# MoBA's scores and its PV products each in one run per layer, in a two-layer hybrid decoder trunk on one Trainium2 core

## The chip, the cores and the metric

The kernel runs on one core of a Trainium2 chip. The metric is the device time of one execution in microseconds (us); less is better. Five engines run side by side, each with its own program: PE (TensorE: matmuls, with weight loads shown apart as PEld), DVE (VectorE), ACT (ScalarE), POOL (GpSimd) and SP (SyncE, which here only issues DMAs). They meet through semaphores.

## The reference

Two layers, 256 tokens, width 1024, one sequence. In each layer one input projection feeds three groups of heads, and each group's output is gated and goes through one output projection:

```
h = rms_norm(x, norm_g[l])
q_a, k_a, v_a, q_h, f_h, i_h, q_m, z = split(h @ w_in[l])      # w_in: 1024 x 5120 -> seven parts of 512 and z of 1536
o_a = moba_attention(rope(norm(q_a)), rope(norm(k_a)), v_a)    # 8 heads x 64
o_h = rms_norm(hgrn2_chunkwise(q_h, f_h, i_h, lb))             # 4 heads x 128, a gated linear recurrence
o_m = memory_attention(norm(q_m), km, vm)                      # 4 heads x 128, keys and values from mem
x = x + (concat(o_a, o_h, o_m) * silu(z)) @ w_out[l]           # w_out: 1536 x 1024
```

MoBA lets a query see its own block of 256 keys, causally, and the best of the blocks that lie wholly in the past. With 256 tokens there is one block, so what is computed is causal attention: scores `q k^T`, a mask, softmax, and the product of the probabilities P with v (PV).

## The kernel before

**The stream of weights.** Every projection is done in three passes on weights and activations that are split into a high and a low part. A chunk of weights, 128 x 1024 f32 (512 KB), is loaded by SP (`wr`, L178), cast by ACT to its high part (`wh`, L214, or L218 with a gain), and the rest is taken by DVE (`wl`, L228 or L232). A layer has 60 such chunks: behind those of the memory's keys and values come, four each, HGRN's forget gate and q, MoBA's k, HGRN's i, MoBA's q, the gate of HGRN's branch (zh), the memory's q (qm), MoBA's v (va), the gates of MoBA's and of the memory's branch, and 12 of w_out. There are 4 buffers of raw chunks; the look-ahead is 5 chunks for loads, 3 for the high and 2 for the low part.

**Who sets the order.** `group_a` and `group_b` issue the projection matmuls (L276, 128x512 or 128x256, 128 rows by 128 columns of the array); `w_out_phase` issues those of the output projection (L1261). After each part they call `slot()`, which lets every waiting generator (`spawn`, `yield`, `reach(l, c)`: "from chunk c of layer l on") do its next piece. A scheduler then fixes each engine's program from this order and its own estimate of times; `mm_row` (L280) keeps a matmul at its place in the written order, `in_turn` adds edges that only order instructions of one engine, `issue_after` puts one instruction behind another. PSUM has 8 banks of 128x512: 4 `acc` for projections, 4 `sd` for all else.

**MoBA.** `g_moba` starts when q and k are normed and turned. Heads come in two units of 4; tokens t = 0 and t = 1 are the two halves of the sequence. The scores are f32 matmuls on 64 of the array's rows, two heads beside each other: 8 of 128x128 for t = 0 of all heads, then 4 of 128x256 for t = 1 of unit 0 (`second(0)`), all in four `sd` tiles. `g_moba_unit` of unit 1 issues its own 4 (`second(1)`) when two `sd` tiles are free again. DVE adds the mask and takes the maximum in one instruction (`masked`, L1033), then the bias `nba`; ACT takes the exponentials (L1068), DVE scales them (L1076) and transposes P in blocks of 32 (`blk`, L95). `across` sends `blk` through DRAM on POOL's queue: one store (L106), 768 KB, and four loads (L111) into `PT`. The PV products use 64 of the array's columns, again two heads beside each other: for each head one of 128x256 and one of 128x128, into one `sd` tile a unit. Unit 0's come from chunk 48 on, where the last projection has been issued, unit 1's from chunk 50 on, so in the middle of w_out. `y_store` gates the product and splits it for w_out (`ys`, `yh`, `yl`, L782 to L784).

**HGRN's output** `zh` takes the same way through DRAM (`y_turned`): its store and loads stand on POOL's queue between those of the first P (`turned0`) and those of the second (`turned1`), whose store waits for zh's loads to be issued (`behind=f"zh{l}moved"`). Transposed, zh is cast by ACT (L129) just ahead of w_out, whose first four chunks are HGRN's (`KT_ORDER` 4 to 7, then MoBA's 0 to 3, then the memory's 8 to 11). HGRN's matmuls with `ih` on one side and `hST` or `hX` on the other are f32 on the full array.

**The memory's attention** (`g_qm`, `g_mem_unit`) norms qm, scores it against the memory's keys, takes maxima on DVE (`mxm`, L1179), exponentials on ACT (L1186), and has its PV in the later part of w_out.

The functions that the change touches, and what calls them:

Of the kernel before, what the change touches and what calls it, by code (L numbers as in the profile page):

```python
# [28 lines left out]
EPS = 1e-6  # L29
# [16 lines left out]
def hymba_kernel(ctx: ExitStack, tc: tile.TileContext, x, mem, mem_t, positions, w_in, w_out, w_mem_kv,  # L46
# [41 lines left out]
    def across(dst, src, n, stage=None, free=None, name=None, q=None, behind=None):  # L88
        q = q or nc.sync
        if stage is None:  # L90
# [4 lines left out]
        nc.vector.transpose(blk.rearrange("p c (n i) -> p c n i", n=n),  # L95
                            src.rearrange("p (n c i) -> p c n i", n=n, c=4))
# [8 lines left out]
        with tc.issue_after(T[behind].ins) if behind is not None else nullcontext():  # L105
            q.dma_start(there.rearrange("q j c r -> (q j) c r"), blk)  # L106
        if stage is None:
            rel("blk")
        yield 4
        for c in (0, 2, 1, 3):  # L110
            ins = q.dma_start(dst[c * 32:c * 32 + 32], there[:, :, c].rearrange("q j r -> j q r"))  # L111
            if c == 2:
                yield
# [4 lines left out]
    def turned(a, stage=None, q=None, name=None):  # L118
        yield from across(a.rearrange("p (q r) -> p q r", q=4), a, 8, stage, q=q, name=name)
# [7 lines left out]
    def unstripped_high(oh, a):  # L127
        for t in range(2):
            T["ACT"] = nc.scalar.copy(strip_of(oh, t), strips(a)[:, :, t])  # L129
            tc.keep_in_program_order(T["ACT"])  # L130
# [76 lines left out]
    def h_to(n):  # L207
        while st["h"] < min(n, len(chunks)):
# [3 lines left out]
            if g is None:  # L212
                with behind("ACT"):
                    nc.scalar.copy(whs[i], raws[i])  # L214
            else:
                for sl in parts(i):
                    with behind("ACT"):
                        nc.scalar.activation(whs[i][:, sl], raws[i][:, sl], AF.Copy, scale=gT[:, g:g + 1])  # L218
# [119 lines left out]
    def group_a(thl, each):  # L338

        pair = None  # L340
        for h in range(4):
# [12 lines left out]
            spawn(g_sum(h, pair[:, (h % 2) * 256:(h % 2) * 256 + 256], acc, each(h - 1, pair) if h % 2 else None))  # L354
            slot(True)

    def g_sum(h, o, acc, then):
        lo = sb.tile([128, 256], F32, name="al", tag="al", bufs=2)
        nc.scalar.copy(lo, acc[:, 256:])
        N["sum", h] = T["sum"] = nc.vector.tensor_tensor(o, acc[:, :256], lo, op=OP.add)  # L360
# [262 lines left out]
    def sumsq(dst, acc, n):  # L623
        sq = sb.tile([128, 512], F32, name="sq", tag="sq", bufs=2)
        nc.scalar.activation(sq, acc, AF.Square)
        nc.vector.tensor_reduce(dst, heads(sq, n), AX.X, OP.add)

    def rsq(name, ss, n, width):
        ms = small(name + "m", n)
        nc.vector.tensor_scalar(ms, ss, 1.0 / width, EPS, op0=OP.mult, op1=OP.add)  # L630
# [116 lines left out]
    def g_va(l, acc):  # L747
        T["va"] = sb.tile([128, 2, 512], F32, name="va", tag="hq1", bufs=1)
        for t in range(2):
            nc.scalar.copy(T["va"][:, t], acc[t])  # L750
# [11 lines left out]
    def g_zt(l, br, h0, acc):  # L762
# [3 lines left out]
        with tc.issue_after(T["exp"].ins):  # L766
            nc.scalar.activation(sg, acc, AF.Sigmoid)
# [10 lines left out]
    def y_store(l, br, u, po):  # L778
        yh, yl = (a.rearrange("p k s -> p (k s)")[:, u * 512:(u + 1) * 512] for a in y_tiles(br))
        ys = sb.tile([128, 512], F32, name="ys", tag="sq", bufs=2)  # L780
        with tc.issue_after(T["sum"].ins):
            nc.vector.tensor_tensor(ys, po, zT[br][:, u * 512:(u + 1) * 512], op=OP.mult)  # L782
        nc.scalar.copy(yh, ys)
        nc.vector.tensor_tensor(yl, ys, yh.bitcast(F32), op=OP.subtract)  # L784
# [4 lines left out]
    def y_turned(l):  # L789
# [3 lines left out]
        yield from turned(flat, "hq0", nc.gpsimd, f"zh{l}")  # L793
# [9 lines left out]
    def g_hgrn(l):  # L803
# [145 lines left out]
        for t in range(2):  # L949
# [8 lines left out]
            sumsq(ss[:, t * 4:t * 4 + 4], o, 4)  # L958
# [3 lines left out]
        for t in range(2):  # L962
            for h in range(4):
                z = zh[:, t, h * 128:(h + 1) * 128]
                nc.vector.scalar_tensor_tensor(z, in0=po[t][:, h * 128:(h + 1) * 128],
# [65 lines left out]
    def masked(P, i, t, s, mx):  # L1031
        c, nk = t * 4 + i, 128 * (t + 1)
        nc.vector.tensor_tensor_reduce(out=P[:, i, kc[t]], in0=s, in1=cm[:, 256 - nk:], scale=1.0, scalar=-3e38,  # L1033
# [3 lines left out]
    def second(u):  # L1037
        qT, kT = T["qT"], T["kT"]
        ps = [side_tile() for _ in range(2)]
# [6 lines left out]
    def second_masked(u, ps, P, mx):  # L1046
# [3 lines left out]
        rel("sd", 2)  # L1050

    def g_moba_unit(l, u, P, mx):
# [9 lines left out]
        nc.vector.tensor_tensor(nb.rearrange("p (t h) -> p t h", t=2), mx.rearrange("p (t h) -> p t h", t=2),  # L1062
                                nr.rearrange("p (t h) -> p t h", t=2)[:, :, 4 * u:4 * u + 4], op=OP.mult)
        yield
        for t in range(2):
            for i in range(4):
                c, r = t * 4 + i, t * 8 + 4 * u + i
                nc.scalar.activation(P[:, i, kc[t]], P[:, i, kc[t]], AF.Exp, bias=nb[:, c:c + 1],  # L1068
                                     scale=rq[:, r:r + 1], accum_out=sm[:, c:c + 1])
            yield  # L1070
        yield
        nc.vector.reciprocal(ri, sm)
        for t in range(2):
            for i in range(4):
                c = t * 4 + i
                nc.vector.tensor_scalar(P[:, i, kc[t]], P[:, i, kc[t]], ri[:, c:c + 1], None, op0=OP.mult)  # L1076
# [5 lines left out]
                          behind=f"zh{l}moved" if u else None)  # L1082
        yield from reach(l, (48, 50)[u])
# [15 lines left out]

    def g_moba(l):  # L1100
# [9 lines left out]

        yield from room("sd", 4)
        ps = [side_tile() for _ in range(2)]
# [272 lines left out]
```

## Time and profile before

| | |
|---|---|
| three runs | 390.16, 389.32, 389.84 us; median 389.84 |
| the profiled execution | 390.01 us, its span 388.2 us |
| granted TensorE clock | 1.000 |
| PE busy, matmul records | 382.4 us, 2455 |
| DVE, ACT, POOL busy | 320.5, 247.6, 85.3 us |
| HBM | 74.60 MB read, 9.44 MB written, 216 GB/s |

A row of the timeline gives start, length, engine, line, operation, output and inputs, the part of the array (rows * columns), the shape, and the number of instructions that follow each other. The length of a matmul is that of its passage through the array, which overlaps with the next one's; what a matmul costs is the step from one start to the next. An f32 matmul shows as two records, and a row's line can be L276 or L280 for the same kind of matmul, since both lines only wrap the call.

### The profile page before, as it was taken

How to read it: one execution, taken by the hardware profiler on the slowest of the kernel's cores; microseconds unless marked ns; L12 is line 12 of the kernel's file. 1: busy time of each engine (PE TensorE's matmuls, PEld its weight loads, DVE VectorE, ACT ScalarE, POOL GpSimd, SP SyncE). 2: the span in 40 equal slices, each digit the busy share in tenths (PEclk: the TensorE clock that was granted, in tenths of full speed). 3: DMA queues.
4: the chain of work that ended last, by engine and by line, in shares of the span. 5: the costliest groups of instructions: out<-in, count | busy, mean ns of one | idle time of the engine just before them, and what ended most of it. 6: DMA issues, size and time to landing. Idle time of an engine off the chain costs nothing.

```text
span 388.2 us, 6790 instructions
## 1 busy us (share of the span) xinstructions
PE 382.4 (98%) x2455; PEld 319.2 (82%) x2455; DVE 320.5 (83%) x621; ACT 247.6 (64%) x414; POOL 85.3 (22%) x129
## 2 busy tenths in 40 slices
PE   7999999999999999999999999999999999999996
PEld 5888888788888888788888888888888889887885
DVE  4789899999659999958577689899696699998663
ACT  5988755567768849754375756445765984785540
POOL 3004400434202623400000040014062054252000
PEclk9999999999999999999999999999999999999999
DMA  8985595439534999985465568736866179999512
GB/s 266 417 307 181 188 320 181 162 113 312 177 108 140 289 289 365 286 258 176 155 210 164 175 206 234 254 110 180 252 191 195 54 255 275 322 335 280 175 39 108
DMA packets 26241, 84.48 MB, mean 218 GB/s; under 512 B 3552, under 2 KB 5984, under 8 KB 26208
## 3 DMA queue, kind: packets, MB, share of 16 engines
q1 hardware_dynamic: 22304, 71.31, 55.7%
q0 software_dynamic: 3616, 12.59, 10.4%
q8 instruction: 19, 0.31, 0.3%
q10 hardware_dynamic: 288, 0.15, 0.1%
q14 instruction: 14, 0.11, 0.1%
HBM read 74.60 MB, written 9.44 MB: 216 GB/s over the span
## 4 chain that ended last, share of the span: by engine, by line
PE 97%; DMA 1%; DVE 0%; SPq 0%; ACT 0%; issue 0%; DVEq 0%
PE acc L276 69%; PE acc L1261 17%; PE sd L276 6%; PE sd L280 4%; DMA wr<-in_w_mem_kv_dram 1%; PE sd L489 1%; PE sd L1017 0%; PE sd L1147 0%; SPq L178 0%; ACT wh L218 0%; DVE xs L1305 0%; DVE xs L1312 0%; DVEq L1312 0%
## 5 line engine op out<-in xcount | busy, mean ns | idle before, releaser
L214 ACT CAST wh<-wr 128x1024 fp32r<-128x1024 f32 x96 | 100.8, 1051 | 68.1 <-PE acc L276 46.8
L228 DVE TENSOR_TENSOR wl<-wr,wh 128x1024 fp32r<-128x1024 f32 x96 | 116.8, 1217 | 26.1 <-ACT wh L214 26.0
L276 PE MATMUL acc<-wh,hT 128*128 128x512 f32 x384 | 122.9, 394 | 0.0
L276 PEld LDWEIGHTS acc<-wh,hT 128*128 128x128 f32 x384 | 71.5, 188 | 15.8 <-issue 0.7
L276 PE MATMUL acc<-wl,hT 128*128 128x512 f32 x192 | 75.6, 394 | 0.0
L276 PE MATMUL acc<-hT,wh 128*128 128x512 f32 x256 | 64.8, 392 | 0.0
L276 PEld LDWEIGHTS acc<-hT,wh 128*128 128x128 f32 x256 | 46.0, 189 | 8.4 <-ACT kn L639 0.4
L276 PEld LDWEIGHTS acc<-wl,hT 128*128 128x128 f32 x192 | 36.1, 188 | 7.3
L1261 PE MATMUL acc<-wh,yl 128*128 128x512 f32 (+1 forms) x96 | 37.2, 387 | 0.0
L1261 PE MATMUL acc<-wl,yh 128*128 128x512 f32 (+1 forms) x96 | 37.2, 387 | 0.0
L232 DVE SCALAR_TENSOR_TENSOR wl<-wr,gT,wh 128x1024 fp32r<-128x1024 f32 (+1 forms) x29 | 31.2, 1096 | 7.1 <-ACT wh L218 7.0
L276 PEld LDWEIGHTS acc<-hT,wl 128*128 128x128 f32 x256 | 34.9, 190 | 2.5
L218 ACT ACTIVATE wh<-wr,gT 128x1024 fp32r<-128x1024 f32 (+1 forms) x29 | 28.3, 1000 | 12.4 <-PE acc L1261 4.1
L276 PE MATMUL acc<-hT,wl 128*128 128x256 f32 x256 | 35.7, 282 | 0.0
L1261 PE MATMUL acc<-wh,yh 128*128 128x512 f32 (+1 forms) x96 | 33.1, 392 | 0.0
L276 PE MATMUL acc<-wh,mTh 128*128 128x512 f32 x64 | 25.3, 399 | 1.2 <-ACT wh L218 0.9
L276 PE MATMUL acc<-wh,mTl 128*128 128x512 f32 x64 | 24.8, 390 | 0.0
L982 POOL TENSOR_TENSOR rka<-msa,pw 128x8 f32<-128x8 f32 x4 | 9.9, 2475 | 58.2 <-DVE msa L981 58.2
L1068 ACT ACTIVATE P<-P,nba,rq 128x128 f32<-128x128 f32 (+1 forms) x32 | 17.1, 537 | 8.3 <-DVE nba L1062 8.3
L1261 PEld LDWEIGHTS acc<-wh,yh 128*128 128x128 f32 x96 | 18.0, 188 | 4.1 <-issue 0.7
L1261 PEld LDWEIGHTS acc<-wh,yl 128*128 128x128 f32 x96 | 18.0, 188 | 3.7
L1261 PEld LDWEIGHTS acc<-wl,yh 128*128 128x128 f32 x96 | 18.0, 188 | 3.5
(219 smaller groups left out, 589.2 us busy)
## 6 DMA issues: line engine op xcount, KB each, us to landing
wr<-in_w_in_dram SPq DMA_DIRECT2D x80, 512.0 KB, 3.7
wr<-in_w_out_dram SPq DMA_DIRECT2D x24, 512.0 KB, 6.0
wr<-in_w_mem_kv_dram SPq DMA_DIRECT2D x15, 512.0 KB, 4.4
there<-blk POOLq DMA_DIRECT2D x4, 768.0 KB, 5.5
PT<-there POOLq DMA_DIRECT2D x16, 192.0 KB, 4.8
there<-blk POOLq DMA_DIRECT2D x6, 512.0 KB, 5.3
there<-blk SPq DMA_DIRECT2D x4, 512.0 KB, 2.9
P<-there POOLq DMA_DIRECT2D x16, 128.0 KB, 6.9
```

The costliest lines, as they stand in the source:

```text
L214: nc.scalar.copy(whs[i], raws[i])
L218: nc.scalar.activation(whs[i][:, sl], raws[i][:, sl], AF.Copy, scale=gT[:, g:g + 1])
L228: N["wl", i] = nc.vector.tensor_tensor(wls[i], raws[i], whs[i].bitcast(F32), op=OP.subtract)
L232: ins = nc.vector.scalar_tensor_tensor(wls[i][:, sl], in0=raws[i][:, sl], scalar=gT[:, g:g + 1], in1=whs[i][:, sl].bitcast(F32), op0=OP.mu ...
L276: nc.tensor.matmul(o, lhsT=a, rhs=b, start=s, stop=e)
L280: tc.keep_in_program_order(nc.tensor.matmul(o, lhsT=a, rhs=b, start=s, stop=e))
L489: ins = nc.tensor.transpose(pt[:, j * 256 + t * 128:j * 256 + (t + 1) * 128], xn[t][:, k * 128:(k + 1) * 128], ident)
L982: nc.gpsimd.tensor_tensor(r[:, t8], ms[:, t8], pw[:, :8], op=OP.pow)
L1068: nc.scalar.activation(P[:, i, kc[t]], P[:, i, kc[t]], AF.Exp, bias=nb[:, c:c + 1], scale=rq[:, r:r + 1], accum_out=sm[:, c:c + 1])
L1261: ins = nc.tensor.matmul(a, lhsT=y, rhs=wt[:, cs], start=n == (0 if to is None else nk - 2) and j == 0, stop=n == nk - 1 and j == 2)
```

## The change

- **Scores.** `second(u, ps)` is given its tiles. Unit 1's scores for t = 1 are issued right behind unit 0's, into two `acc` tiles instead of `sd` tiles; so `g_moba` now waits until the memory's q projection is under way (chunk 32) and the gates of zh are done. All masks stand in one place, unit 0's, then unit 1's.
- **PV.** Unit 0's generator ends when its P is on its way. Unit 1's issues all 16 matmuls, from chunk 48 on, ahead of w_out, into two `sd` tiles, each matmul kept in the written order; then both units' `y_store`.
- **The way through DRAM.** The second P's store goes behind zh's store instead of zh's loads, and zh's loads go behind the second P's store.
- **Orders.** Three tables of `in_turn` hold DVE's and ACT's order in the attention, the memory's attention and w_out. In the program ACT's order comes out as it was. On DVE, unit 1's masks and `nba` come up beside unit 0's, and the second P's transposition goes ahead of the first maximum `mxm` that stood ahead of it.

On PE, where the scores of the first layer stand. Before, in two places (`kT`, `qT` are MoBA's, `wh`, `wl` the weights, `hT` the activations):

```order
L276 MATMUL acc<-wh,hT 128x512
L280 MATMUL sd<-kT,qT 128x128 x8
L280 MATMUL sd<-kT,qT 128x256 x4
L276 MATMUL acc<-wh,hT 128x512
L276 MATMUL acc<-wl,hT 128x512
```

```order
L276 MATMUL acc<-wl,hT 128x512
L276 MATMUL acc<-wh,hT 128x512
L280 MATMUL sd<-kT,qT 128x256 x4
L276 MATMUL acc<-wh,hT 128x512
L276 MATMUL acc<-wl,hT 128x512
```

And after, in one place:

```order
L282 MATMUL acc<-wh,hT 128x512
L286 MATMUL sd<-kT,qT 128x128 x8
L286 MATMUL sd<-kT,qT 128x256 x4
L286 MATMUL acc<-kT,qT 128x256 x4
L282 MATMUL acc<-wh,hT 128x512
L282 MATMUL acc<-wl,hT 128x512
```

The second place's four matmuls moved to the first. The lines are 6 higher in the changed file. HGRN's run with `ih`, which stood whole between the two places, is cut in two by 6 projection matmuls.

On PE, unit 1's PV of the first layer. Before, in the middle of w_out (`yh`, `yl` are the gated outputs); unit 0's same eight stood ahead of w_out:

```order
L1261 MATMUL acc<-wl,yh_1883 128x512
L1261 MATMUL acc<-wh,yl_1884 128x512
L280 MATMUL sd<-PT,va 64x256
L276 MATMUL sd<-PT,va 64x128
L276 MATMUL sd<-PT,va 64x256
L276 MATMUL sd<-PT,va 64x128
L276 MATMUL sd<-PT,va 64x256
L276 MATMUL sd<-PT,va 64x128
L276 MATMUL sd<-PT,va 64x256
L276 MATMUL sd<-PT,va 64x128
L1261 MATMUL acc<-wh,yh_1883 128x512
```

And after, the end of the run, whose first eight rows are unit 0's, up to w_out's first matmul:

```order
L286 MATMUL sd<-PT,va 64x256
L286 MATMUL sd<-PT,va 64x128
L286 MATMUL sd<-PT,va 64x256
L286 MATMUL sd<-PT,va 64x128
L286 MATMUL sd<-PT,va 64x256
L286 MATMUL sd<-PT,va 64x128
L286 MATMUL sd<-PT,va 64x256
L286 MATMUL sd<-PT,va 64x128
L1297 MATMUL acc<-wh,yh_1893 128x512
L1297 MATMUL acc<-wl,yh_1893 128x512
```

Unit 1's eight matmuls moved from behind w_out's first chunks to ahead of all of w_out.

On POOL, the queue of the three transfers in the first layer (128x1536 is a P, 128x1024 is zh; `nrm` is a scale of the memory's scores). Before:

```order
L106 DMA there<-blk 128x1536
L632 TENSOR_TENSOR hgr<-hgm,pw 128x8
L111 DMA PT<-there 32x4x384 x4
L632 TENSOR_TENSOR qmr<-qmm,pw 128x8
L106 DMA there<-blk 128x1024
L1138 TENSOR_SCALAR nrm<-qmr 128x8
L111 DMA zh<-there 32x4x256 x4
L106 DMA there<-blk 128x1536
L111 DMA PT<-there 32x4x384 x4
```

And after:

```order
L106 DMA there<-blk 128x1536
L638 TENSOR_TENSOR hgr<-hgm,pw 128x8
L117 DMA PT<-there 32x4x384 x4
L638 TENSOR_TENSOR qmr<-qmm,pw 128x8
L1148 TENSOR_SCALAR nrm<-qmr 128x8
L106 DMA there<-blk 128x1024
L106 DMA there<-blk 128x1536
L117 DMA zh<-there 32x4x256 x4
L117 DMA PT<-there 32x4x384 x4
```

The second P's store moved ahead of zh's loads, and `nrm` ahead of zh's store.

The diff, without the edits that only name an instruction for `in_turn`, and with a line or two of each of its tables:

```diff
@@ across
-    def across(dst, src, n, stage=None, free=None, name=None, q=None, behind=None):
+    def across(dst, src, n, stage=None, free=None, name=None, q=None, behind=None, loads_behind=None):
...
         with tc.issue_after(T[behind].ins) if behind is not None else nullcontext():
-            q.dma_start(there.rearrange("q j c r -> (q j) c r"), blk)
+            ins = q.dma_start(there.rearrange("q j c r -> (q j) c r"), blk)
+        if name is not None:
+            T[name + "stored"] = ins
+            done.add(name + "stored")
         if stage is None:
             rel("blk")
         yield 4
+        while loads_behind is not None and loads_behind not in done:
+            yield
         for c in (0, 2, 1, 3):
-            ins = q.dma_start(dst[c * 32:c * 32 + 32], there[:, :, c].rearrange("q j r -> j q r"))
+            with tc.issue_after(T[loads_behind].ins) if loads_behind is not None else nullcontext():
+                ins = q.dma_start(dst[c * 32:c * 32 + 32], there[:, :, c].rearrange("q j r -> j q r"))
@@ y_turned
-        yield from turned(flat, "hq0", nc.gpsimd, f"zh{l}")
+        yield from turned(flat, "hq0", nc.gpsimd, f"zh{l}", f"turned1{l}stored")
@@ second, second_masked
-    def second(u):
+    def second(u, ps):
         qT, kT = T["qT"], T["kT"]
-        ps = [side_tile() for _ in range(2)]
...
-        rel("sd", 2)
+        N["first mask", u], N["last mask", u] = N["mask", 4], N["mask", 7]
@@ g_moba_unit
-        if u:
-            yield from room("sd", 2)
-            ps = second(u)
-            yield
-            second_masked(u, ps, P, mx)
...
-                          behind=f"zh{l}moved" if u else None)
-        yield from reach(l, (48, 50)[u])
+                          behind=f"zh{l}stored" if u else None)
+        T["PT", u] = PT
+        if u == 0:
+            return
+        yield from reach(l, 48)
         while f"va{l}" not in done or f"z{A_}{l}" not in done:
             yield
         va = T["va"]
-        yield from room("sd")
-        po = side_tile()
-        for i in range(4):
-            h = 4 * u + i
+        yield from room("sd", 2)
+        pos = [side_tile() for _ in range(2)]
+        for h in range(8):
+            v, i = divmod(h, 4)
             rows, c = slice(64 * (i % 2), 64 * (i % 2) + 64), (i // 2) * 256
-            pieces = PT.rearrange("p q (n s) -> p n q s", n=12)[:, 3 * i:3 * i + 3]
-            o = po[rows, c:c + 256].rearrange("p (b q s) -> p b q s", b=2, q=4)
-            (mm if i else mm_row)(o, va[:, 0, h * 64:(h + 1) * 64], pieces[:, 0:2], True, False)
-            mm(o[:, 1], va[:, 1, h * 64:(h + 1) * 64], pieces[:, 2], False, True)
-        rel(tag)
-        yield
-        y_store(l, A_, u, po)
+            pieces = T["PT", v].rearrange("p q (n s) -> p n q s", n=12)[:, 3 * i:3 * i + 3]
+            o = pos[v][rows, c:c + 256].rearrange("p (b q s) -> p b q s", b=2, q=4)
+            mm_row(o, va[:, 0, h * 64:(h + 1) * 64], pieces[:, 0:2], True, False)
+            mm_row(o[:, 1], va[:, 1, h * 64:(h + 1) * 64], pieces[:, 2], False, True)
+        rel("PTh")
+        rel("PTl")
+        yield
+        for v in range(2):
+            y_store(l, A_, v, pos[v])
+            yield
@@ g_moba
+        yield from reach(l, 32)
+        while f"z{H_}{l}" not in done:
+            yield
         yield from room("sd", 4)
+        first = [side_tile() for _ in range(2)]
         ps = [side_tile() for _ in range(2)]
...
-        ps1 = second(0)
-        yield
-        for p in range(4):
-            for e in range(2):
-                masked(P[p // 2], p % 2 * 2 + e, 0, ps[e][:, p * 128:(p + 1) * 128], mx[p // 2])
-        rel("sd", 2)
-        second_masked(0, ps1, P[0], mx[0])
+        seconds = [second(0, first), second(1, [acc_tile() for _ in range(2)])]
+        yield
         for u in range(2):
-            yield
+            for p in (2 * u, 2 * u + 1):
+                for e in range(2):
+                    masked(P[u], p % 2 * 2 + e, 0, ps[e][:, p * 128:(p + 1) * 128], mx[u])
+            second_masked(u, seconds[u], P[u], mx[u])
+            rel("sd", 2)
             spawn(g_moba_unit(l, u, P[u], mx[u]))
+            yield
@@ order_of_attention, order_of_memory, w_out_phase
+        in_turn(("last mask", 0), ("nba", 0), ("first mask", 1), ("last mask", 1), ("nba", 1), w("wl", 36), ("ria", 0),
...
+                ("across", f"turned1{l}"), ("mxm", 0, 0), w("wl", 42), ("mxm", 1, 0), w("wl", 43))
...
+        in_turn(("wh", first + 3), ("yh", A_, 0), ("wh", first + 4), ("yh", A_, 1), ("wh", first + 5))
```

More of the change, by code (lines that the diff above doesn't have):

```diff
@@ L94, in across @@
         blk = sb.tile([128, 4, n * 32], F32, name="blk", tag=tag, bufs=1)
-        nc.vector.transpose(blk.rearrange("p c (n i) -> p c n i", n=n),
-                            src.rearrange("p (n c i) -> p c n i", n=n, c=4))
+        N["across", name] = nc.vector.transpose(blk.rearrange("p c (n i) -> p c n i", n=n),
+                                                src.rearrange("p (n c i) -> p c n i", n=n, c=4))
         if free is not None:
@@ L116, in across, with turned @@
             done.add(name + "moved")
-    def turned(a, stage=None, q=None, name=None):
-        yield from across(a.rearrange("p (q r) -> p q r", q=4), a, 8, stage, q=q, name=name)
+    def turned(a, stage=None, q=None, name=None, loads_behind=None):
+        yield from across(a.rearrange("p (q r) -> p q r", q=4), a, 8, stage, q=q, name=name, loads_behind=loads_behind)
     def strips(a):
@@ L128, in unstripped_high @@
         for t in range(2):
-            T["ACT"] = nc.scalar.copy(strip_of(oh, t), strips(a)[:, :, t])
+            T["ACT"] = N["yh", t] = nc.scalar.copy(strip_of(oh, t), strips(a)[:, :, t])
             tc.keep_in_program_order(T["ACT"])
@@ L213, in h_to @@
                 with behind("ACT"):
-                    nc.scalar.copy(whs[i], raws[i])
+                    N["wh", i] = nc.scalar.copy(whs[i], raws[i])
             else:
@@ L336, in group_kv, with group_a @@
             slot(True)
-    def group_a(thl, each):
+    def group_a(thl, each, of=None):
         pair = None
@@ L353, in group_a, with g_sum @@
                 pair = sb.tile([128, 512], F32, name="as", tag="as", bufs=2)
-            spawn(g_sum(h, pair[:, (h % 2) * 256:(h % 2) * 256 + 256], acc, each(h - 1, pair) if h % 2 else None))
+            spawn(g_sum(of, h, pair[:, (h % 2) * 256:(h % 2) * 256 + 256], acc, each(h - 1, pair) if h % 2 else None))
             slot(True)
-    def g_sum(h, o, acc, then):
+    def g_sum(of, h, o, acc, then):
         lo = sb.tile([128, 256], F32, name="al", tag="al", bufs=2)
-        nc.scalar.copy(lo, acc[:, 256:])
-        N["sum", h] = T["sum"] = nc.vector.tensor_tensor(o, acc[:, :256], lo, op=OP.add)
+        N["al", of, h] = nc.scalar.copy(lo, acc[:, 256:])
+        N["sum", of, h] = N["sum", h] = T["sum"] = nc.vector.tensor_tensor(o, acc[:, :256], lo, op=OP.add)
         if then is not None:
@@ L749, in g_va @@
         for t in range(2):
-            nc.scalar.copy(T["va"][:, t], acc[t])
+            N["va", t] = nc.scalar.copy(T["va"][:, t], acc[t])
         yield 2
@@ L1132, in g_qm @@
         for t in range(2):
-            nc.scalar.copy(qm[:, t], acc[t])
+            N["qm", t] = nc.scalar.copy(qm[:, t], acc[t])
         for t in range(2):
-            sumsq(ss[:, t * 4:t * 4 + 4], acc[t], 4)
+            sumsq(ss[:, t * 4:t * 4 + 4], acc[t], 4, "qm", t)
         r = rsq("qm", ss, 8, 128)
@@ L1192, in g_mem_unit @@
         yield
[L1193 removed]
+        N["rim", u] = nc.vector.reciprocal(ri, sm)
         for t in range(2):
@@ L1288, in w_out_phase @@
         i = st["c"]
+        in_turn(("wl", first + 2), ("ys", A_, 0), ("gate", M_, 2), ("wl", first + 3), ("yl", A_, 0), ("wl", first + 4),
+                ("ys", A_, 1), ("yl", A_, 1), ("wl", first + 5))
+        in_turn(("wh", first + 3), ("yh", A_, 0), ("wh", first + 4), ("yh", A_, 1), ("wh", first + 5))
         def put(t, c0, c1):
```

77 lines of the change are left out of this document (51 added, 26 removed).

## The prediction

> **What bounds the kernel now.** I read the page first (shares of the span, the chain that ended last), then the busy time by stretch, then single instructions on the timeline. From the page:
>
> ```profile
> span 388.2 us, 6790 instructions
> PE 382.4 (98%) x2455; PEld 319.2 (82%) x2455; DVE 320.5 (83%) x621; ACT 247.6 (64%) x414; POOL 85.3 (22%) x129
> PE 97%; DMA 1%; DVE 0%; SPq 0%; ACT 0%; issue 0%; DVEq 0%
> ```
>
> PE is busy for 382.4 of 388.2 us, and the chain that ended last is PE's for 97%. The change touches, in each layer, the stretch from the first scores to the first PV product. This is the first layer's, by the windows' columns (span of the stretch, then PE, PEld, DVE, ACT, POOL busy, granted clock, DMA share, GB/s):
>
> ```profile
> 104.00:158.00 54.00, 54.00 (x323) 45.87 (x321) 49.01 (x123) 41.40 (x89) 15.44 (x22) 1.00 0.71 232
> ```
>
> PE is busy in all 54.00 us, at full clock. So nothing is won by an earlier DVE, ACT or DMA: the time falls only if PE has less to do, and rises only if something that PE takes now in time comes late. But PE may be "busy" and yet not at its pace, and that is where the change works. On the timeline, its rows (start, length, form, count) around the second of the two runs of MoBA scores, the 4 matmuls of unit 1, f32, each in two records:
>
> ```profile
> 115.09 0.39 PE L276 MATMUL acc<-wh,hT 128*128 128x512 f32 x1
> 115.41 1.13 PE L280 MATMUL sd<-kT,qT 64*128 64x256 f32 x8
> 116.48 0.50 PE L276 MATMUL acc<-wh,hT 128*128 128x512 f32 x1
> 116.81 0.40 PE L276 MATMUL acc<-wl,hT 128*128 128x512 f32 x1
> ```
>
> From the last projection matmul before the run to the second one after it are 1.72 us (116.81 - 115.09). Two of the steps in it are the projection's own. Its pace comes from a group without a break, 12 matmuls from 137.09 to 139.81, 0.227 each:
>
> ```profile
> 137.09 2.88 PE L276 MATMUL acc<-hT,wh 128*128 128x512 f32 x12
> 139.81 0.40 PE L276 MATMUL acc<-hT,wl 128*128 128x256 f32 x2
> ```
>
> The run thus takes 1.72 - 0.45 = 1.27 us of PE's time. The pace inside it comes from timelines with narrow windows, which cut a group short. The first row is the same run, cut behind 4 of its 8 records; the pair below it is of 128-wide scores, cut behind 6 and behind 12 records:
>
> ```profile
> 115.41 0.70 PE L280 MATMUL sd<-kT,qT 64*128 64x256 f32 x4
> ```
>
> ```profile
> 105.31 0.50 PE L280 MATMUL sd<-kT,qT 64*128 64x128 f32 x6
> 105.31 0.84 PE L280 MATMUL sd<-kT,qT 64*128 64x128 f32 x12
> ```
>
> Four records more lengthen the first by 0.43 us (1.13 - 0.70): a 256-wide matmul, two records, takes 0.215. Six records more lengthen the second by 0.34: a 128-wide one takes 0.113. Four of 256 are 0.86. So 1.27 - 0.86 = **0.41 us** of this run is no matmul: it is the price of changing from full-array matmuls to 64-row ones and back. It shows in the steps: 0.32 at the entry instead of 0.23 (115.09 to 115.41), about 0.2 between the last scores (115.41 + 0.86 = 116.27) and 116.48, and 0.33 instead of 0.23 behind that.
>
> Why there: the weight load. Rows of PEld and PE at the first run's entry:
>
> ```profile
> 104.56 0.19 PEld L276 LDWEIGHTS acc<-wh,hT 128*128 128x128 f32 x1
> 104.78 0.39 PE L276 MATMUL acc<-wh,hT 128*128 128x512 f32 x1
> 105.10 0.30 PEld L280 LDWEIGHTS sd<-kT,qT 64*128 64x128 f32 x4 [0.35 <-ACT sg L757]
> 105.10 2.03 PE L280 MATMUL sd<-kT,qT 64*128 64x128 f32 x24
> ```
>
> Between projections a load starts a whole step (0.22) ahead of its matmul; that of the first 64-row matmul starts together with it, at 105.10. Nothing is loaded ahead across the switch.
>
> **The change part by part. Scores in one run.** The same matmuls as before, but unit 1's four stand behind unit 0's: one entry and one exit fewer, -0.41 us a layer. The second layer's run is as long: 1.06 as a piece of the chain that ended last, where the first layer's is 1.07 from its first record to the next projection (116.48 - 115.41):
>
> ```profile
> 304.44 1.06 PE sd L280 x8
> ```
>
> **PV in one run.** Unit 1's PV now stands in the middle of w_out; rows of both its ends, then its start and end in the second layer:
>
> ```profile
> 163.78 0.39 PE L1261 MATMUL acc<-wh,yl 128*128 128x512 f32 x1
> 164.09 0.43 PE L280 MATMUL sd<-PT,va 128*64 128x256 f32 x1
> 165.59 0.51 PE L1261 MATMUL acc<-wh,yh 128*128 128x512 f32 x1
> 165.94 0.39 PE L1261 MATMUL acc<-wl,yh 128*128 128x512 f32 x1
> ```
>
> ```profile
> 353.05 0.43 PE L280 MATMUL sd<-PT,va 128*64 128x256 f32 x1
> 354.55 0.51 PE L1261 MATMUL acc<-wh,yh 128*128 128x512 f32 x1
> ```
>
> 2.16 us (165.94 - 163.78) less two steps of 0.227 is 1.71. Four matmuls of 256 and four of 128 by the paces above are 0.86 + 0.45 = 1.31. The rest is 0.40 us, and 1.50 from the first PV to the next w_out matmul in both layers. Behind unit 0's PV that goes: -0.40 a layer.
>
> By the Trainium skill, "TensorEngine Tiling (Array Packing)", Key Properties, a change of tiling mode drains TensorE, and "TensorE: Matmul & The Clock Gate", Single matmul latency, gives a matmul 398 cycles beside its columns, at 2.4 GHz 0.166 us. An estimate from the two: 0.33 a run, 1.33 in all, 388.5; the trace agrees in kind and shows 0.41.
>
> **The ih·hST run** of HGRN is now split by projection matmuls. These are full-array f32 matmuls; the entry, in the profile of before:
>
> ```profile
> 111.04 0.39 PE L276 MATMUL acc<-wh,hT 128*128 128x512 f32 x1
> 111.27 1.27 PE L276 MATMUL sd<-ih,hST 128*128 128x128 f32 x10
> ```
>
> 0.23, the projection's own step: a split costs about nothing. Bounds: 0, and a 64-row run's 0.41 a layer; I take 0, the row of the same form.
>
> **DVE.** All of unit 1's masks and its nba move up, beside unit 0's; ACT's order doesn't change. Their thinnest follower is a weight part (wl) that PE takes soon after:
>
> ```profile
> 124.54 1.21 DVE L228 TENSOR_TENSOR wl<-wr,wh 128x1024 fp32r<-128x1024 f32 x1
> 126.16 0.40 PE L276 MATMUL acc<-wl,hT 128*128 128x512 f32 x1
> ```
>
> It ends at 125.75 and is taken at 126.16, 0.41 ahead. PE comes 0.41 earlier, which uses this up and no more; and four masks and the nba that stood ahead of this wl on DVE are gone from there, so that it comes earlier too. I take nothing; if the scores' gain were lost on it altogether, 0.41 a layer. The two tiles of unit 1's scores now come from the projection accumulators, and wait for the gate of zh that frees them:
>
> ```profile
> 105.68 0.68 DVE L759 TENSOR_TENSOR zh<-acc,sg 128x512 f32<-128x512 f32 x1
> ```
>
> Free at 106.36; unit 1's scores come last in the run, at about 107.1 (105.10 + 2.03): 0.7 to spare.
>
> **POOL and the second P.** PV of unit 1 now needs P's transposed copy (PT) 1.31 us behind the first PV's start instead of 7.6: in layer 2 at 353.05 - 7.62 + 1.31 - 0.41 = 346.3 (7.62 is 164.09 less 156.47, the first layer's first PV in the row below). Its path now, in layer 2, and the tile view of PT for all of its loads; last, the reader of the transposed zh:
>
> ```profile
> 156.47 0.43 PE L280 MATMUL sd<-PT,va 128*64 128x256 f32 x1
> 326.68 1.77 DVE L95 STREAM_TRANSPOSE blk<-P 128x1536 f32<-128x1536 f32 x1
> 330.87 0.60 POOL L106 DMA_DIRECT2D there<-blk  x1
> 339.13 2.22 POOL L111 DMA_DIRECT2D PT<-there  x4 [7.66 <-DMA there<-blk]
> DMA to landing us min/median/max: 4.2/4.8/6.0
> 343.74 1.12 ACT L129 CAST yh<-zh 128x512 fp32r<-128x512 f32 x2
> ```
>
> As it stands it could land at 341.35 + 6.0 = 347.3, too late. But P is transposed by 328.45, and its store waited till 330.87 for zh's loads, which it now precedes: 2.4 earlier, so landed by 344.9, 1.4 us in time (more, as the transposition now also stands ahead of a maximum, mxm). What is queued behind that store on POOL, which now waits for P's transposition, are zh's loads: issued from 329.05 (328.45 + 0.60) to some 331.3, landed by 337.3 even at PT's slowest 6.0, and wanted by ACT at 343.74. That hides a store of zh that comes a little later as well. The maximum, behind the transposition, comes up to 1.77 later; on PE the memory group's PV hangs on it, well within w_out. I take nothing for these; were the maximum's cover gone, up to 1.77 a layer.
>
> **The sum.** Two layers by (0.41 + 0.40) = 1.62 us less. The profiled execution took 390.01 (span 388.2 and 1.8 around it): 388.39. The runs' median, 389.84, lies 0.17 lower: **388.2**.
>
> **Rivals.** *Nothing is removed*: the 0.4 is the 64-row matmuls' own, the pipeline filling and emptying, and is paid by the same matmuls wherever they stand. Then 389.8. For it: ends of matmuls are modelled. Against: 0.41 and 0.40 come out of runs with different matmuls, 0.86 and 1.31 us long. The Trainium skill, "TensorE: Matmul & The Clock Gate", Part 3: Packing small matmuls, lets a weight load overlap running matmuls only when its row group differs; by that no full-array load would be ahead, a switch would cost no more than any other load, and the gain would be none. The load at 104.56, 0.22 ahead of its matmul, doesn't agree.
>
> *Half the gain*: PT of unit 1, or its score tiles, come late, and PE empties between the units after all. It keeps one switch of two: 0.81 gained, 389.0.
>
> *Slower: the earlier store delays the weights.* The second P's store, 768 KB, now starts 2.4 us or more earlier, while the last projection weights arrive. The last of them in layer 1, its issue, the landings of that stretch, and who waits for it; last, the store's own landing, from the page:
>
> ```profile
> 141.67 0.33 SPq L178 DMA_DIRECT2D wr<-in_w_in_dram  x1
> DMA to landing us min/median/max: 3.7/5.3/6.9
> 152.01 1.04 ACT L214 CAST wh<-wr 128x1024 fp32r<-128x1024 f32 x1
> 153.59 0.40 PE L276 MATMUL acc<-hT,wh 128*128 128x512 f32 x1
> there<-blk POOLq DMA_DIRECT2D x4, 768.0 KB, 5.5
> ```
>
> It lands by 148.6, 3.4 before ACT's cast, which ends 0.54 before PE wants it. From 3.9 us of delay on PE waits. If it queued behind the whole store (5.5), PE would stand 1.6 us a layer: 3.2 - 1.6 = +1.6, 391.4. Against: the bytes are the same, they only move; the DMA share in the stretch is 0.71; and most of the weights were issued before.
>
> **How the numbers follow.** Forecast 0.72; nothing removed 0.08; half 0.08; slower 0.09; 0.03 for more than the sum. The forecast's own range is 387.6 to 389.0: 0.6 below for the spread of the runs (389.32 to 390.16), above the bound of the split run or of a lost wl (0.82 for two layers, either of them). With the half gain, at 389.0, it holds 0.80, and 0.1 for the place of these ends on each side gives 387.5 to 389.2. A measurement can tell about 0.2%, 0.78 us: faster means below 389.06. The half gain, 0.81, lies on that line and is split: faster 0.72 + 0.04 + 0.03 = 0.79; same 0.08 + 0.04 = 0.12; slower 0.09.
>
> **Signs.** Right: one run of scores of 32 records, by the timeline 2.9 us long (2.03 + 0.86); one PV run, 2.81 us from its first record to the next w_out matmul (1.50 + 1.31); PE's busy time lower by about 1.6 with no idle time in the two stretches; the second P's store ahead of zh's loads on POOL and PT landed before 346. Wrong: a gap or a step of 0.3 in the middle of a merged run (half gain); scores of 3.3 us (2.03 + 1.27) and PV of 3.2 (1.50 + 1.71) (nothing removed); PE idle on a weight cast near 153 and 342 (slower).

## The result, and the profile after

The changed kernel took 392.61 us in the median of six runs (391.01 to 394.03), the kernel before beside it 389.70: a ratio of 1.0071, 95% interval 1.0052 to 1.0089. It is slower, where 388.2 was forecast. Run a second time, in a later set of twelve, it took 389.87 (388.24 to 394.02; ratio 1.0026, 0.9993 to 1.0060). So the change doesn't cost a fixed sum: its best executions are as fast as forecast, its worst 5.8 us slower. One execution of e10 below, 400.69 us at a mean granted clock of 0.982, is left out of its ratio.

The profiled execution took 392.55 us. From its page:

```profile
span 390.7 us, 6781 instructions
PE 382.6 (98%) x2455; PEld 320.9 (82%) x2455; DVE 320.9 (82%) x621; ACT 247.9 (63%) x414; POOL 85.4 (22%) x129
PE 88%; DMA 5%; ACT 4%; issue 1%; DVE 1%; SPq 0%; ACTq 0%; DVEq 0%
```

PE's share of the chain that ended last fell from 97% to 88%; DMA and ACT now have 9%. The pieces of that chain show that the merges are there, and how far apart their places are (start, length, what):

```profile
107.42 1.96 PE sd L286 x24
109.38 0.86 PE acc L286 x8
...
159.43 2.80 PE sd L286 x32
...
178.78 0.12 PE sd L286
```

The same places in the kernel before, the first scores and the memory's PV:

```profile
105.17 1.96 PE sd L280 x24
176.34 0.12 PE sd L280
```

By the chain the scores take 1.96 + 0.86 = 2.82 us, by the timeline's rows 2.89 (107.36 to 110.25), where 2.9 by the timeline was forecast; PV takes 2.80, where 2.81 was. But from the first scores to the memory's PV the first layer took 71.36 us (178.78 - 107.42) where it took 71.17 before, and should have taken 70.36. And already the scores came 2.25 us late. The difference of 2.54 us between the two profiled executions is made of three things: 2.25 ahead of the first scores, some 1.6 gained by the merges, and some 1.9 lost in the two layers.

**The start.** PE's matmul behind the first wait on weights, in the changed kernel and in the one before (the bracket is PE's idle time ahead of it), and the windows' rows for 8 to 12 us, whose seventh number is the granted clock:

```profile
8.17 0.71 PE L282 MATMUL acc<-wh,mTh 128*128 128x512 f32 x1 [1.80 <-ACT wh L224]
```

```profile
8.00:12.00 4.00, 3.83 (x10) 3.02 (x11) 3.68 (x7) 3.39 (x7) 0.00 (x0) 0.57 1.03 415
```

```profile
7.52 0.50 PE L276 MATMUL acc<-wh,mTh 128*128 128x512 f32 x1 [0.90 <-ACT wh L218]
```

```profile
8.00:12.00 4.00, 4.00 (x20) 3.27 (x19) 3.82 (x7) 3.95 (x7) 0.00 (x0) 1.00 1.04 415
```

The second part of the first weights landed 0.65 us later, PE stood 1.80 us instead of 0.90, and then got a clock of 0.57 for four us. The change doesn't touch this part of the program: its instructions are the same, in the same order, on every engine.

**Ahead of PV.** The chain of the changed kernel before the first layer's PV, and the wait that begins it in the second layer:

```profile
140.94 6.75 DMA wr<-in_w_in_dram
...
147.71 0.05 ACT wh L220
...
148.67 2.29 ACT P L1197 x8
...
155.27 1.04 ACT wh L220
...
156.35 3.08 PE acc L282 x16
...
329.49 7.24 DMA wr<-in_w_in_dram
```

A load of weights (the last projection chunk but one, issued at 140.94) lands at 147.69. ACT casts it at once and then, in its fixed order, takes the memory's eight exponentials, a sigmoid and the last chunk's cast, which ends at 156.3; PE stands 0.70 us for it. That idle time is counted from the modelled end of the matmul before. From start to start the step is 0.98 us (155.37 to 156.35) where the steps before it are 0.12, and the next one is 0.34 instead of 0.23: 0.97 us in all. The same cast before, and that chunk's load (one instruction, by the tile view):

```profile
144.45 1.05 ACT L214 CAST wh<-wr 128x1024 fp32r<-128x1024 f32 x1 [1.47 <-PE acc L276]
```

```profile
L178 SPq DMA_DIRECT2D wr<-in_w_in_dram x1: 328/328/328, 138.3 to 138.3; - x1
...
DMA to landing us min/median/max: 5.7/5.7/5.7
```

From this cast to the last chunk's cast it is 7.56 us in both kernels (144.45 to 152.01; 147.71 to 155.27). Before, PE released the first cast; the load had landed at 144.02, only 0.43 ahead. Counted from the first scores, and with the 0.41 by which PE is now earlier, it lands 1.83 us later than before (40.27 - 38.85 + 0.41). Two orders on other engines make that up. DVE and POOL in the changed kernel, then DVE and POOL before:

```profile
137.44 1.77 DVE L95 STREAM_TRANSPOSE blk<-P 128x1536 f32<-128x1536 f32 x1
...
139.71 1.21 DVE L234 TENSOR_TENSOR wl<-wr,wh 128x1024 fp32r<-128x1024 f32 x1
```

```profile
139.51 0.54 POOL L106 DMA_DIRECT2D there<-blk  x1 [4.22 <-DVE blk L95]
140.96 2.24 POOL L117 DMA_DIRECT2D zh<-there  x4 [0.91 <-DMA there<-blk]
```

```profile
137.04 1.21 DVE L228 TENSOR_TENSOR wl<-wr,wh 128x1024 fp32r<-128x1024 f32 x1
...
141.29 0.59 POOL L106 DMA_DIRECT2D there<-blk  x1
```

The wl at 139.71 is the last reader of the raw buffer that the load needs (140.92 to 140.94). The second P's transposition now stands ahead of it, so the load is issued 0.82 late (140.94 - 138.28 - 2.25 + 0.41). And the second P's store, issued at 139.51, is now ahead of the load instead of 3.0 behind it (141.29 against 138.28): the load takes 6.75 instead of 5.74. What the two queues moved from 141.2 to 142.7 us in the changed kernel (q0 has POOL's transfers, q1 SP's; packets, MB, share):

```profile
q0 software_dynamic: 97, 0.60, 100.9%
q1 hardware_dynamic: 7, 0.00, 0.3%
```

The store went first, and the weights, issued at 140.94, moved nothing until it was nearly through.

### The profile page after: what moved, and what is told of

Same layout as the page of the kernel before. It is cut to its first block, busy times and chain, and to the rows that moved or that the text cites. A ratio compares the mean times of both kernels' runs of the same rounds, so it can differ in the third digit from the quotient of the medians.

```text
span 390.7 us, 6781 instructions
## 1 busy us (share of the span) xinstructions
PE 382.6 (98%) x2455; PEld 320.9 (82%) x2455; DVE 320.9 (82%) x621; ACT 247.9 (63%) x414; POOL 85.4 (22%) x129
## 4 chain that ended last, share of the span: by engine, by line
PE 88%; DMA 5%; ACT 4%; issue 1%; DVE 1%; SPq 0%; ACTq 0%; DVEq 0%
PE acc L282 61%; PE acc L1297 17%; PE sd L282 5%; PE sd L286 4%; DMA wr<-in_w_in_dram 4%; ACT P L1197 2%; DMA wr<-in_w_mem_kv_dram 1%; PE sd L495 1%; ACT L773 1%; ACT wh L220 1%; PE sd L1157 0%; PE sd L1023 0%; PE acc L286 0%; DVE wl L234 0%; SPq L184 0%
## 5 line engine op out<-in xcount | busy, mean ns | idle before, releaser
L282 PE MATMUL acc<-wl,mTh 128*128 128x512 f32 x64 | 21.0, 407 | 0.0
```

The lines of the kernel that those rows point to most:

```text
L282: nc.tensor.matmul(o, lhsT=a, rhs=b, start=s, stop=e)
```

## The experiments

Theory A: the loss is this load, made late by DVE's order and by the store ahead of it, and the merges bring what was forecast. Rival B: the merges themselves set ACT back. Rival C: without the early store the second P comes late. For the start, S: the clock falls because PE stands too long; S1, that this start belongs to the program, S2, to single executions.

| kernel | median, us | kernel before beside it | ratio, 95% interval |
|---|---|---|---|
| changed (result) | 392.61 | 389.70 | 1.0071, 1.0052 to 1.0089 |
| e1 store back | 387.64 | 389.44 | 0.9949, 0.9932 to 0.9965 |
| e2 DVE back | 387.76 | 389.44 | 0.9968, 0.9951 to 0.9985 |
| e3 both back | 387.68 | 389.44 | 0.9955, 0.9939 to 0.9972 |
| e4 changed, start filled | 389.81 | 389.44 | 0.9998, 0.9981 to 1.0014 |
| e5 changed, again | 389.87 | 389.61 | 1.0026, 0.9993 to 1.0060 |
| e6 scores merged only | 389.02 | 389.61 | 0.9985, 0.9971 to 0.9998 |
| e7 PV merged only | 388.67 | 389.61 | 0.9974, 0.9959 to 0.9990 |
| e8 both back, start filled | 388.20 | 389.61 | 0.9965, 0.9948 to 0.9982 |
| e9 changed, 5 raw buffers | 387.87 | 389.42 | 0.9966, 0.9949 to 0.9983 |
| e10 e1 and one more store | 390.28 | 389.42 | 1.0026, 0.9997 to 1.0056 |
| e11 both back, 5 raw buffers | 387.50 | 389.42 | 0.9948, 0.9927 to 0.9969 |
| e12 changed, store held back | 388.09 | 389.60 | 0.9953, 0.9933 to 0.9974 |

**e1: POOL's order back.**

```diff
-        yield from turned(flat, "hq0", nc.gpsimd, f"zh{l}", f"turned1{l}stored")
+        yield from turned(flat, "hq0", nc.gpsimd, f"zh{l}")
...
-                          behind=f"zh{l}stored" if u else None)
+                          behind=f"zh{l}moved" if u else None)
```

> The changed kernel, with POOL's order as it was: zh's loads ahead of the second P's store. Theory A (late weights): in the changed kernel the raw chunk whose cast begins ACT's last chain before w_out lands 1.8 us later than before, measured from the scores: 0.8 of it because it is issued later (the second P's transposition stands ahead of the wl that frees its buffer), 1.0 because its transfer shares the DMA engines with the second P's store. It had about 1.0 to spare, so PE stands 0.7 us a layer. With the store back, 0.8 of lateness is left, under the 1.0: no idle time of PE before PV, about 2.0 us less than the changed kernel, 390.5 with the same start and 388.3 with a start at full clock. Theory B (the merges themselves set ACT back): no change, 392.5, PE still idle by 0.7 on the cast in both layers. Theory C (the second P comes late without the early store): the cast is in time, but PE stands in the middle of the PV run.

387.64; PE has no wait on a cast in either layer, nor in the PV run. The late chunk's load, by the tile view:

```profile
L184 SPq DMA_DIRECT2D wr<-in_w_in_dram x1: 327/327/327, 138.2 to 138.2; - x1
...
DMA to landing us min/median/max: 4.5/4.5/4.5
```

B falls: the merges are all there. So does C: the early store isn't needed, the second P's last load landed at 155.0, and the PV run began at 155.7, with the second P's part 1.3 us behind that.

**e2: DVE's order back.**

```diff
-                ("across", f"turned1{l}"), ("mxm", 0, 0), w("wl", 42), ("mxm", 1, 0), w("wl", 43))
+                ("mxm", 0, 0), w("wl", 42), ("mxm", 1, 0), ("across", f"turned1{l}"), w("wl", 43))
```

> The changed kernel, with the second P's transposition behind the two maxima and their wl on DVE, as it was; POOL's order stays changed. Theory A: the raw chunk is issued up to 1.8 us earlier, and the store, which waits for the transposition, starts later; the lateness falls under the 1.0 to spare: PE idle by 0 to 0.3 us a layer, 1.4 to 2.0 us less than the changed kernel. Theory B: PE still idle by 0.7 in both layers, 392.5.

387.76, no wait in the traced execution, though five of the eleven runs lay over 388 (up to 389.71). The load is issued at 136.4, 2.6 us ahead of the store, and lands in 4.4.

**e3: both orders back**, the two edits together.

> The changed kernel, with both orders back, DVE's and POOL's: only the merges are left. Theory A: no idle time of PE on the cast, and the four removed switches show whole: 388.2 with a start at full clock, 390.5 with the changed kernel's start. Theory C: the second P's loads land after unit 1's PV could start (the profile of before had them land at 155.3 and 345.5, where it would now start at 157.4 and 346.3): little or no wait in layer 1, up to 0.5 us in layer 2. Theory B: 392.5.

387.68, no wait, though four of its eleven runs lay over 388 (up to 389.55), and there is no trace of those (e9's, below, is of such a run of a like kernel). To put either order back is enough. DVE's lateness alone, 0.82 us, stays under the 0.97 that was spare (e1). With DVE's order back the load goes out ahead of the store as well (e2), so no run has the early store without DVE's lateness. The stretch from the first scores to the memory's PV, by the chain of this kernel:

```profile
104.34 1.96 PE sd L286 x24
...
174.72 0.12 PE sd L286
```

70.38 us against 71.17 before: 0.79 a layer, 1.58 in all, where 1.62 was forecast.

**e4: the changed kernel, its start filled.** Eight more empty matmuls behind the first four real ones:

```diff
+WARM2 = 8
...
+                if i == 0 and g == 0 and t == 1:
+                    pt = side_tile()
+                    for _ in range(WARM2):
+                        mm(pt[:, :256], zb[:, :128], zb, True, True)
+                    rel()
```

> The changed kernel, with 8 more of the empty bf16 matmuls behind the first four real ones, in the gap in which PE waits for the second part of the first weights (1.80 us in the changed kernel's profile, 0.90 in that of before). Theory S (the granted clock falls to 0.57 from 8 to 12 us because PE stands too long in that gap): the clock stays at 1.000, the stretch to the first scores is 1.6 us shorter, 391.0. Rival (the clock falls for another reason): it falls again, 392.5.

The clock was 1.00 from 8 to 12 us and the scores came at 104.09, 3.3 us earlier than in the changed kernel. This doesn't test S: the empty matmuls came out directly behind the first 17, ahead of the real ones, and in this execution the weights landed at 5.6 instead of 7.4 us, so that there was no gap. Still the profiled execution took 391.74, since the load of the late chunk, 1.4 us behind the store, took 8.3 us in the first layer, and PE stood 2.27 us. Without a slow start, then, the changed kernel still loses.

**e5: the changed kernel again**, unedited.

> The changed kernel itself once more, beside the kernel before and the next three. In its first profile 2.25 us of its 392.55 were lost ahead of the scores, in a start at a granted clock of 0.57 from 8 to 12 us. If that start belongs to the program (theory S1), it comes again: a clock of 0.994 to 0.996 in every run and 392.5. If it belongs to single executions or to the conditions of the first runs (theory S2), it comes seldom, and what is left is the loss ahead of PV: 387.7 (the kernel with both orders back) plus 0.7 to 1.0 us a layer, 389.1 to 389.8, like the changed kernel with the filled start (389.81). PE waits for a weight cast ahead of PV in at least one layer in both cases.

S1 falls: this profiled execution of the same program started at full clock, with the scores at 105.13. Four of the 35 runs of the kernel before in this set had a mean clock of 0.995 or 0.996, at 391.6 to 391.9, with no wait of its own later on; that these were such starts is likely, not shown, as no trace of them was taken. The wait ahead of PV came again, larger, in the first layer alone. The load, its wait, and the clock from 150 to 158 us:

```profile
L184 SPq DMA_DIRECT2D wr<-in_w_in_dram x1: 328/328/328, 138.6 to 138.6; - x1
...
DMA to landing us min/median/max: 8.2/8.2/8.2
```

```profile
155.54 2.85 PE L282 MATMUL acc<-hT,wh 128*128 128x512 f32 x7 [2.19 <-ACT wh L220]
```

```profile
150.00:158.00 8.00, 5.82 (x28) 4.81 (x27) 7.72 (x17) 7.97 (x19) 1.25 (x2) 0.88 0.90 282
```

Behind this wait of 2.19 us the granted clock was lower as well (0.77 from 154 to 158 us, 0.80 from 158 to 162), 0.996 in the mean of the whole execution, and this layer's stretch was 74.37 us, 4.0 over e3's. Three more of the twelve runs had 0.990 to 0.996, at 393.3 to 394.0. The second layer's load took 5.9 us, and its stretch was 70.36, without loss.

**e6 and e7: one merge each**, with both orders back. e6 has the PV of before (unit 1's from chunk 50 on, one `sd` tile a unit); e7 has the scores of before.

```diff
+        yield from reach(l, (48, 50)[u])
...
+        po = side_tile()
+        for i in range(4):
```

> The scores merged, the orders of DVE and POOL back, and PV in two runs again (unit 1's from chunk 50 on). By the price of a switch, 0.40 us a run and layer, it loses 0.81 to the kernel with both merges: 388.5, with two PV pieces of 1.50 us in a layer instead of one of 2.80. Rival (a run costs nothing of its own): 387.7.

```diff
+        if u:
+            yield from room("sd", 2)
+            ps = second(u, [side_tile() for _ in range(2)])
+            yield
+            second_masked(u, ps, P, mx)
```

> PV merged, the orders of DVE (but for unit 1's masks, which go with its scores) and POOL back, and the scores in two runs again. By the price of a switch, 0.41 us, 388.5, with scores of 1.96 and 1.06 us instead of 2.82. Rival (a run costs nothing of its own): 387.7.

The medians lie 0.8 and 0.5 over e8's, run beside them. The stretch, which the starts don't touch, is sharper; e6, then e7:

```profile
105.59 1.96 PE sd L286 x24
...
176.43 0.12 PE sd L286
```

```profile
104.93 1.96 PE sd L286 x24
...
175.66 0.12 PE sd L286
```

70.84 and 70.73, against 71.17 before: 0.33 for the scores, 0.44 for PV, together 0.77, and 0.79 with both. Each run costs its own switch.

**e8: both orders back, the start filled**, e3 with e4's edit (and its 8 matmuls at the same place).

> Both merges, both orders back, and the 8 empty matmuls in the gap of the start. If short starts were already full speed in the kernel with both orders back, no change: 387.5 to 387.7, a clock of 1.000. If some of its executions lost clock at the start (it had runs up to 389.55), the spread of the runs falls and the highest comes under 388.5.

388.20 (387.82 to 388.98), in a set where the kernel before had 389.61: not faster than e3, whose traced start was already at full clock. The highest run is lower than e3's, and over 388.5 all the same.

**e9: the changed kernel with `RAW_BUFS` 5 instead of 4.**

> The changed kernel, both of its orders as changed, with 5 buffers for raw weights instead of 4: the load of the chunk that came late needs no longer wait for the wl behind the second P's transposition and one maximum, but for the wl before it, and is issued some 3 us earlier, ahead of the second P's store. Theory A (the chunk comes late because it is issued behind that transposition and then shares the DMA engines with the store): no wait of PE on a cast ahead of PV, and the time falls to that of the kernels with an order back, 387.7 to 388.2, with few runs over 390. Rival (it is the DMA traffic of the stretch alone, however early the chunk is issued): the transfer takes 6 to 8 us as in the changed kernel, PE still waits, 389.8.

387.87, no wait ahead of PV in the traced execution. The load goes out at 135.9, 2.0 us ahead of the store, and lands in 3.9; the next chunk's, behind the store, takes 7.4 and has the time. Five of the twelve runs took 388.9 to 389.6, and the traced one, 389.01, is of these: its stretches are 70.36 and 70.37 us, as short as e3's, but its first scores come at 105.79 instead of 104.34. So the 1.44 us that it has over e3's traced execution lie ahead of the scores.

**e10: e1 with one more store of 768 KB**, of x, behind zh's first load.

```diff
+            if c == 0 and name is not None and name.startswith("zh"):
+                more = away.tile([4, 32, 4, 384], F32, name="more", tag="more", bufs=1)
+                with tc.issue_after(ins.ins):
+                    T["more"] = nc.gpsimd.dma_start(more..., xs[:, :, :768])
+                loads_behind = "more"
```

> The kernel with POOL's order back (DVE's order as changed, 387.64), with one more store of 768 KB behind the first of zh's four loads, of x from SBUF to a place that nobody reads; the output stays the same. It starts within about 1 us of the late chunk's load, as the second P's store does in the changed kernel. Theory A (the transfer shares the DMA engines with a 768 KB store): the chunk's transfer takes 6.5 us or more instead of 4.5, PE waits for a cast ahead of PV again, by 0.5 to 2 us in a layer, 388.7 to 391. It also delays the second P, whose store and loads stand behind it on the queue, so PE may wait in the PV run as well. Rival (the store costs the chunk nothing; the loss came from DVE's order alone): 387.6.

Slower than e1 (387.64), but not by the wait that I expected. The store was issued at 137.95, the chunk's load 0.13 us ahead of it, and it took 4.5; the next chunk's, 1.6 behind, took 9.0. What came late was the second P, in the middle of the PV run:

```profile
155.25 1.57 PE L292 MATMUL sd<-PT,va 128*64 128x256 f32 x16
159.26 1.11 PE L292 MATMUL sd<-PT,va 128*64 128x256 f32 x10 [2.44 <-DMA PT<-there]
```

By 141.1 us the extra store had moved nothing, and four fifths of the load's 0.52 MB had gone. From 139.3 to 141.1 the only queue with packets was SP's:

```profile
q1 hardware_dynamic: 101, 0.41, 74.6%
```

So this run doesn't show what traffic beside the load costs; it agrees with the load being late by what goes ahead of it. That gave the last experiment its form.

**e11: e3 with 5 raw buffers.**

> Both merges, both orders back, 5 buffers for raw weights. In the kernel with both orders back nothing waits ahead of PV, so by theory A no gain in the best runs (387.5), but perhaps fewer slow ones (4 of its 11 runs lay over 388).

387.50 (387.16 to 388.13), the lowest median, though with seven runs not told apart from e3. The spread of 0.97 us is smaller than e3's 2.10, not than e1's 0.64.

**e12: the changed kernel, its store held back.** Twelve small multiplications on POOL read the transposed P ahead of the store:

```diff
+        if name is not None and name.startswith("turned1"):
+            for n in range(12):
+                late = small("late", 8)
+                with tc.issue_after(T[behind].ins):
+                    T["late"] = nc.gpsimd.tensor_tensor(late, blk[:, 0, :8], pw[:, :8], op=OP.mult)
+                behind = "late"
```

> The changed kernel in all its orders, with 12 small multiplications on POOL ahead of the second P's store (they read its transposed P and write to a tile that nobody reads). They should hold the store, and zh's loads behind it, back by 1.5 us or more, so that the late chunk's load, which was issued 1.3 to 1.4 us behind the store, now is issued ahead of it. Nothing else moves: DVE's order and with it the chunk's issue stay late by 0.8 us. Theory A, sharpened (what counts is whether the chunk is issued ahead of the store or behind it: 3.9 to 4.7 us to landing in four profiles where it was ahead, 6.75 to 8.3 where it was behind): the chunk lands in 4 to 5 us, no wait of PE on a cast ahead of PV, and a median of 387.6 to 388.2, 1.7 to 2.3 us below the changed kernel's 389.87. Rival (the change loses by DVE's order or by the traffic of the whole stretch): the waits stay, 389.5 to 390; a later store may also bring the second P too late for PV.

388.09. POOL spent 3.9 us on them and issued the store at 140.12, 2.2 behind the chunk's load, which then took:

```profile
L190 SPq DMA_DIRECT2D wr<-in_w_in_dram x1: 328/328/328, 137.9 to 137.9; - x1
...
DMA to landing us min/median/max: 3.1/3.1/3.1
```

No wait on a cast; PE stood 0.44 us in the first layer's PV run for the second P instead, and the second layer's run took 3.19 us by the timeline instead of 2.87. So the stretches were 71.06 and 70.71 us. Even so the later store is 1.8 us better than the earlier one (389.87).

## Why the prediction was wrong

- **The switches: right.** 2.82 and 2.80 us for the merged runs, 1.58 us gained where 1.62 was summed (0.33 and 0.44 a layer for 0.41 and 0.40, when done apart). Splitting the run with `ih` cost nothing that shows: its two pieces are 0.89 and 1.78 us, together 2.67 where it was 2.68. PE's busy time, another of the signs, fell by 1.8 us where no low clock lengthens it (380.6 in e3, 382.4 before). The stretch was 70.36 to 70.39 us in both layers of e1, e2, e3, e9 and e11. "Nothing is removed" fell.
- **"POOL and the second P": the step that failed.** It looked for what waits behind the moved store on POOL's queue, and found zh's loads, which had time. It didn't ask which loads of SP's queue are issued behind the store. Issued ahead of it, the late chunk's load landed in 3.1 to 5.7 us (both layers of before, e1 to e3 and e6 to e12); in the changed kernel, e4 and e5, 1.3 to 1.4 behind it, in 5.9 to 8.3. It also took the maximum's lateness, "up to 1.77", for the memory's PV alone. Behind that maximum on DVE stands a wl, and its end frees a raw buffer, so SP's load was moved too.
- **The slower rival had the place and the mechanism, and the wrong chunk.** It named PE's idle time on a cast near 153 and 342, and it came at 156 and 345. But it counted the cover of the last chunk, issued at 141.67: 3.4 us. The cast that sets the time is the one before it: ACT's order fixes 7.56 us from there to the last cast, and its load had 0.43 us to spare, with the 0.54 behind the last cast 0.97 in all. I had read "<-PE acc" at that cast and not asked what was second. With lateness 1.83, 0.9 a layer is lost; 0.98 and 0.92 were measured (71.36 and 71.30 against 70.38). The rival's 5.5 us, a load behind the whole store, was too much: behind it this load took 1.0 to 2.6 us longer than the same layer's before.
- **"PT comes late": wrong for this change**, but e10 and e12 show it at 2.44 and 0.44 us when the store is later still. The early store was reckoned to bring the second P 2.4 us earlier; counted from the first scores, the last of its loads landed 0.4 us earlier than in e1 in the first layer (49.96 against 50.32) and 1.7 in the second (48.07 against 49.77).
- **The range** had no room for a start with late weights and a low clock, 2.25 us in the profiled execution. It isn't the change's: e5's profile of the same program has none. So of the 2.9 us between the two medians of the result a part is not the change's cost. How large a part in those six runs stays open, as only one of them was traced; their mean clocks were 0.994 to 0.998, where eight of e5's twelve had 0.998 or more; by e5 the changed kernel stands at 1.0026 of the kernel before (0.9993 to 1.0060), and 0.7% over e3 (1.0026 by 0.9955).

## What to carry to other kernels

A run of half-array matmuls between full-array ones had here a price of its own, some 0.4 us at both lengths (0.86 and 1.31 us of matmuls); merging such runs was worth just that much (0.33 and 0.44). Before a large transfer is moved ahead, list for every queue the loads that will now be issued behind it, and for each the cover along the whole fixed order of the engine that takes it, not just its first reader's. Where a trace names one releaser, look up when the second was ready: here it was only 0.43 us earlier.

## What the runs showed of the hardware

The late chunk's load, on SP's queue, landed in 3.1 to 5.7 us where it was issued ahead of a 768 KB store on POOL's, and in 5.9 to 8.3 where it was issued 1.3 to 1.4 us behind one. An issue isn't yet a start: e10's extra store was issued at 137.95 and had moved nothing by 141.1. Nor does the order of these two alone set the time. The next chunk's load took 4.6 to 7.9 us where it was issued 0.2 to 0.7 us ahead of the store (before, e3, e6, e7 and e12). Shortly before it the late chunk's load had been issued, and in all but e12 zh's loads too. The Trainium skill, "DMA: Bandwidth & Descriptors", Queues, rings and completion order, has each DMA engine take turns between queues, a packet at a time. The trace agrees with that in e10 from 146.5 to 149.0 us, where POOL's queue moved 105 packets and SP's 103. The 97 against 7 of the changed kernel, from 141.2 to 142.7, are no such turns; whether SP's queue had work ready then, no run here shows.

The granted clock fell behind some waits of PE of about 2 us and not behind others: 1.80 at the start (0.57 from 8 to 12 us), 2.19 in e5 and 2.27 in e4 ahead of PV (0.69 from 153 to 158 us in e4); but it stayed at 1.00 behind 1.62 at the start of e6 and behind the 2.44 in e10. So S is possible and not settled. The Trainium skill, "TensorE: Matmul & The Clock Gate", Part 1, puts the fall at an idle window of about 3.4 us that runs freely of the program; the trace agrees that waits of like length can go either way, and shows falls behind shorter waits than that.
